# Expert products in a mixture-of-experts block: gate and up laid side by side, 512 columns wide

## The chip, the cores and the metric

One NeuronCore of a Trainium2 chip runs the whole program. Its engines work side by side and wait for each other by semaphores: TensorE (PE) multiplies matrices and writes into PSUM banks of 512 columns, VectorE (DVE) and ScalarE (ACT) work elementwise, GpSimd (POOL) does the rest and issues the gathers from DRAM, SyncE (SP) issues the loads. The metric is the device time of one execution in microseconds (us).

## The reference, cut to what matters

The reference is a stack of four attention layers and then a block with a mixture of experts over 256 tokens of 1024 features. Each token goes to 8 of 64 experts. The change touches only the experts' part:

```
hg = jnp.einsum('cd,edf->cef', xc, w_eg)      # gate, D=1024 -> F=256
hu = jnp.einsum('cd,edf->cef', xc, w_eu)      # up,   D=1024 -> F=256
a = jax.nn.silu(hg) * hu * gch[..., None]
return jnp.einsum('cef,efd->cd', a, w_ed)     # down, F=256 -> D=1024
```

## The kernel before, in words

Everything up to the experts (some 888 us) is left as it is by the change. In the experts' part the tokens are sorted into units. Each expert's three matrices lie in DRAM as one row of 3 x 2048 columns per partition: piece 0 is gate, piece 1 is up, piece 2 is down, 1 MB each. There are two kinds of unit, and the routing of this input makes 16 of the first and 22 of the second.

**Big units** (`unit`, up to 128 places of one expert, 16 run, one after the other, each behind a branch in `chain`). A weight piece is loaded in two halves into `eraw`, split by ACT (`hi`, L1847) and DVE (`lo`, L1850) into two parts, and multiplied three times (hi x hi, hi x lo, lo x hi). `wide(u, a, c)` (L1898) makes gate for c = 0 and up for c = 1 from piece c, over all eight row blocks k of 128 features; each matmul has 256 columns. Around the two wide products TensorE turns the former unit's result (`turn`, L1904), adds the unit before that one into the output (`combine`, L1923), multiplies the former unit by its down matrix (`down`, L1917), and turns the next unit's rows (`cols`, L1889). Those rows come by a gather that GpSimd issues (`fetch`, L1882, into `xr`) at the start of the unit ahead of the one that uses them. Order on TensorE: wide 0, turn, combine 0, wide 1, cols 0, combine 1, down 0, cols 1, places, down 1.

**Pairs** (`pair`, two units of at most 64 places side by side in the two column halves of the array, 11 pairs here). The weights are used unsplit. A ring of 11 buffers of 1 MB holds pieces; `load_p(p, j)` loads piece j // 2 of expert j % 2. `wide_p` (L2058) makes gate and then up, 16 matmuls of 256 columns per call, each of which the profile shows as two instructions. `gather_p` (L2049) makes two of the eight row blocks of a later group's input per call, by a product with a one-hot matrix into a PSUM bank, which `copy` moves to `xs` (L273 on ACT, L275 on DVE). `turn_p` (L2064) turns the activation, ACT copies it to `ats` (L2065); `places_p` (L2034, L2036) turns the one-hots, and `down_p` (L2073) multiplies by down. `gather_p`, `turn_p` and `places_p` each take a bank from `tbank`, which hands out two PSUM banks in turn. The experts' part runs under a manual schedule: instructions stand on each engine as they are written, and the framework adds the semaphores that reads and writes of a tile need. In `pair` the gate's `silu` (L2090, ACT) is written behind the gate's product, so that it runs beside the up product, and `av` (L2095, DVE) behind the up product.

Of the kernel before, what the change touches and what calls it, by code (L numbers as in the profile page):

```python
# [13 lines left out]
AF = mybir.ActivationFunctionType  # L14
# [4 lines left out]
P = 128  # L19
S = 256  # L20
D = 1024
KT = D // P
# [3 lines left out]
E = 64  # L26
# [5 lines left out]
def cols_chunk(w, cols, k0=0, nk=8):  # L32

    c = w[k0 * P:(k0 + nk) * P][:, cols]
    return c.reshape(nk, P, c.shape[1]).transpose(1, 0, 2).reshape(P, -1)


def rng(a, n):
    return np.arange(a, a + n)
# [95 lines left out]
def wkey(key, inputs):  # L135
    a = inputs[key]
    return a.reshape(a.shape[-2], a.shape[-1])


def lay_out(inputs):  # L140

    x = {}
    g = {k: np.asarray(v) for k, v in inputs.items()}
    x["w_all"] = np.concatenate(
        [cols_chunk(wkey(key, g), cols, k0, nk).ravel() for _, key, cols, k0, nk in CHUNKS])
    eg = g["w_exp_gate_2"][0].reshape(E, 8, P, 256).transpose(0, 2, 1, 3)
    eu = g["w_exp_up_2"][0].reshape(E, 8, P, 256).transpose(0, 2, 1, 3)
    ed = g["w_exp_down_2"][0].reshape(E, 2, P, D).transpose(0, 2, 1, 3)
    x["w_exp"] = np.concatenate([eg.reshape(E, P, 2048), eu.reshape(E, P, 2048), ed.reshape(E, P, 2048)], axis=2)
    x["x"] = g["x"].reshape(2, P, D)  # L150
    x["pos"] = np.ascontiguousarray(g["positions_2"].reshape(2, P).T)

    def col(a):
        return a.reshape(-1, P).T

    x["cols"] = np.concatenate([
        col(g["c_2"].reshape(-1)),
        col(g["b_ada_2"].reshape(-1)),
        col(g["g_norm1_2"].reshape(-1)),
        col(g["g_norm2_2"].reshape(-1)),  # L160
        g["a_cmp_pos_k"][0].reshape(16, 2, 64).transpose(1, 2, 0).reshape(P, 16),
        g["a_cmp_pos_v"][0].reshape(16, 2, 64).transpose(1, 2, 0).reshape(P, 16),
        np.tile(g["g_na_q_2"].reshape(64, 1), (2, 1)),
        np.tile(g["g_na_k_2"].reshape(64, 1), (2, 1)),
        col(g["g_q_lat_2"].reshape(-1)),
        col(g["g_kv_lat_2"].reshape(-1)),
        np.tile(g["g_mla_q_2"].reshape(-1), 2)[:P].reshape(P, 1),
        np.tile(g["g_mla_k_2"].reshape(-1), 2)[:P].reshape(P, 1),
    ], axis=1)
    x["rows"] = np.concatenate([  # L170
        g["norm_pre"], g["norm_post"], g["g_norm2_2"],
    ], axis=0)
    x["small"] = np.concatenate([g["b_lambda"].reshape(-1), g["b_sub_gain"].reshape(-1), g["e_bias_2"].reshape(-1)])
    x["w2k"] = cols_chunk(wkey("a_cmp_w2_k", g), rng(0, 64), 0, 2)
    x["w2v"] = cols_chunk(wkey("a_cmp_w2_v", g), rng(0, 64), 0, 2)

    rq, cq = np.divmod(np.arange(P), 64)
    j = np.arange(-2, 4)
    ck = np.arange(64)
    dr = j[None, :] - rq[:, None] + 7  # L180
    dc = np.clip(ck[None, :] - cq[:, None], -15, 15) + 15
    rpb = g["na_rpb_2"][0]
    x["na_bias"] = rpb[:, dr[:, :, None], dc[:, None, :]].transpose(1, 0, 2, 3).reshape(P, -1)
    x.update(constants())
    return {k: np.ascontiguousarray(v) for k, v in x.items()}


def constants():
    c = {}
    p = np.arange(P)[:, None]  # L190
    k = np.arange(S)[None, :]
    dist = P + p - k
    big = np.float32(BIG)
    n = np.arange(16)[None, :]
    q = np.arange(P)
    cs = np.clip(q % 64 - 8, 0, 48)[:, None]
    ck = np.arange(64)[None, :]
    inv = (np.float32(10000.0) ** (-np.arange(16, dtype=np.float32) / np.float32(16))).astype(np.float32)
    cmp = [i * P + p - (16 * n + 31) for i in range(2)]

    def put(name, *t):
        c[name] = np.concatenate([np.broadcast_to(a, (P, np.shape(a)[-1])) for a in t], axis=1).astype(np.float32)

    put("consts", np.eye(P), np.where(dist >= 0, dist, big),
        *[np.where((d >= 0) & (n < 15), d, big) for d in cmp],
        np.where(p >= 31, 1.0, 0.0),
        np.where((ck >= cs) & (ck < cs + 16), 0.0, BIG), inv[None])
    put("consts_c", *[np.where((dist >= 0) & (dist % d == 0) & (dist <= w), dist, big) for w, d in ((128, 1), (512, 4), (2048, 16))])
    put("consts_d", np.where(q[:, None] >= q[None, :], -1.0, 0.0), np.full((P, P), -1.0))
    rest = np.where(q >= E, 128.0, 0.0)[None]  # L210
    put("consts_r", np.where(q[:, None] < q[None, :], 1.0, 0.0),
        127.0 - q[None], 127.0 - p, rest, rest.T, rest + 999.0, np.concatenate([np.arange(Kernel.NB), np.arange(Kernel.NS)])[None], p % E)
    put("consts_e", q[None] - 999.0, q[None] % E - 999.0)
    return c
# [18 lines left out]
class Kernel:  # L233
# [1562 lines left out]
    def units(self, num, hn, y):  # L1796
# [3 lines left out]
        nc, tc = self.nc, self.tc  # L1800
# [13 lines left out]
        xs = [mp.tile([P, KT, S], F32, name=f"xs{i}") for i in range(2)]  # L1814
# [6 lines left out]
        sv = mp.tile([P, 256], F32, name="sv")  # L1821
# [30 lines left out]
        def w(j, nk):  # L1852
            return [hl[q][j].rearrange("p (k c) -> p k c", k=nk) for q in range(2)]
# [37 lines left out]
            self.split(x[0], x[1], b.rearrange("p (k n) -> p k n", k=4))  # L1891

        def wide(u, a, c):
            ww = w(c, KT)
            for k in range(KT):
                x = [t[:, k, (u % 2) * P:(u % 2 + 1) * P] for t in self.x]
                for j, (q, p) in enumerate(((0, 0), (0, 1), (1, 0))):
                    nc.tensor.matmul(a[:, c * 256:(c + 1) * 256], x[p], ww[q][:, k, :],  # L1898
                                     start=(k == 0 and j == 0), stop=(k == KT - 1 and j == 2))

        def turn(u):
# [18 lines left out]
        def combine(u, hf, t=None):  # L1920
            for tt in range(2):
                for p in range(2):
                    nc.tensor.matmul(y[tt][hf], (t or pt[u % 5])[:, tt * P:(tt + 1) * P], yo[p][:, 512 * hf:512 * hf + 512],  # L1923
                                     start=False, stop=False, skip_group_check=True)

        def unit(u):
# [8 lines left out]
            if u:  # L1935
                for h in range(2):
                    hi(2, h)
                    lo(2, h)
                    load(u, 2, h)
            a = self.abank()  # L1940
            wide(u, a, 0)
            if u:
                turn(u - 1)
# [4 lines left out]
            for h in range(2):  # L1948
                hi(0, h)
                lo(0, h)  # L1950
                load(u + 2, 0, h)
            wide(u, a, 1)
            if not u:
                places(0)
# [60 lines left out]
        def ring(p, j):  # L2015
            return R[(6 * p + j) % 11]

        def load_p(p, j):
            nc.sync.dma_start(ring(p, j), weights(NB + 2 * p + j % 2, j // 2))
# [31 lines left out]
            self.copy(xs[g % 2][:, k0:k0 + 2, :], b.rearrange("p (k n) -> p k n", k=2), eng)  # L2051

        def wide_p(p, a, c):
            t = [ring(p, 2 * c + e).rearrange("p (k c) -> p k c", k=KT) for e in range(2)]
            for k in range(KT):
                for e in range(2):
                    s = p % 2 * P + 64 * e
                    nc.tensor.matmul(a[64 * e:64 * e + 64, c * 256:(c + 1) * 256], xs[p // 2 % 2][:, k, s:s + 64], t[e][:, k, :],  # L2058
                                     start=(k == 0), stop=(k == KT - 1))

        def turn_p(p):
            b = self.tbank()
            for f in range(2):
                nc.tensor.transpose(b[:, f * P:(f + 1) * P], av[:, f * P:(f + 1) * P], self.ident)  # L2064
            nc.scalar.activation(ats[p % 2], b[:, :S].rearrange("p (f t) -> p f t", f=2), AF.Copy)  # L2065
# [11 lines left out]
        def pair(p, more):  # L2077
            g, i = divmod(p, 2)
            steps = [4 * i, 4 * i + 2] if more and g + 1 < NP // 2 else []
            gath = lambda e: steps and gather_p(g + 1, steps.pop(0), e)  # L2080
            if more:
                for j in range(5):
                    load_p(p + 1, j)
                if i == 0 and g + 2 < NP // 2:
                    onehot_p(g + 2)
            a = self.abank()
            wide_p(p, a, 0)
            if more:
                load_p(p + 1, 5)
            nc.scalar.activation(sv, a[:, 0:256], AF.Silu)  # L2090
            if p:
                combine(p - 1, 0)
            gath("a")
            wide_p(p, a, 1)
            V.tensor_tensor(av, a[:, 256:512], sv, OP.mult)  # L2095
            if p:
                combine(p - 1, 1)
            turn_p(p)
            gath("v")
            places_p(p)  # L2100
            for hf in range(2):
                down_p(p, hf)
            if not more:
                for hf in range(2):
                    combine(p, hf)
# [101 lines left out]
```

## Time and profile before

| | before |
|---|---|
| median of 3 runs (lowest, highest) | 1284.9 us (1281.04, 1289.26) |
| the profiled execution's own time | 1287.51 us |
| its span, first to last instruction | 1285.8 us |
| PE busy | 1214.1 us, 94% |
| PEld (weight load, beside PE) busy | 1040.0 us, 81% |
| DVE busy | 950.7 us, 74% |
| ACT busy | 695.0 us, 54% |
| DMA in the pairs (1120.3 to 1259.6 us) | 395 GB/s, engines busy 0.97 of the time |

The share of busy time is an average over stages with different limits, so each stage is read by itself. The time of a matmul row is that of the whole passage through the array; what a matmul costs in a row of matmuls is the distance from its start to the next one's start.

### The profile page before, as it was taken

What the parts mean: (1) busy time and instruction counts of PE and PEld (TensorE: products, weight loads), DVE (VectorE), ACT (ScalarE), POOL (GpSimd) and SP (SyncE); (2) the same over time, 40 slices, a digit from 0 to 9 for tenths busy, and PEclk for the clock granted to TensorE, in tenths of its full rate; (3) what the DMA queues carried; (4) which work ended last, traced back from release to release, by engine and by line L of the source; (5) the groups of instructions that cost most, each with busy time, mean ns of one, the idle gap of its engine ahead of it and who ended that gap; (6) DMA issues with size and microseconds to landing.
All of it is one profiled execution on the core that took longest, in us unless ns stands there. A gap on an engine that the chain in (4) does not pass through costs nothing. (4 is left out here: it accounts for less than half of the span.)

```text
span 1285.8 us, 23661 instructions
## 1 busy us (share of the span) xinstructions
PE 1214.1 (94%) x8366; PEld 1040.0 (81%) x8366; DVE 950.7 (74%) x2363; ACT 695.0 (54%) x1509; POOL 223.2 (17%) x295
## 2 busy tenths in 40 slices
PE   5899998999989999999989999989899998999996
PEld 5888876998879987999878898878889887666663
DVE  6977889879997788888689689878889887211123
ACT  5667785456645554468665555543767766211111
POOL 2034411001100110002100000023335344011100
PEclk9988998999989999999999999999999999899998
DMA  8461205664357644866444235335888887999991
GB/s 298 165 235 34 99 34 166 252 238 158 109 188 283 226 139 144 320 249 250 148 170 169 85 115 174 131 145 195 324 310 286 296 306 271 381 418 403 414 403 48
DMA packets 54802, 282.19 MB, mean 219 GB/s; under 512 B 5920, under 2 KB 6720, under 8 KB 29952
## 3 DMA queue, kind: packets, MB, share of 16 engines
q1 hardware_dynamic: 48784, 261.98, 55.1%
q0 software_dynamic: 4000, 15.44, 3.4%
q10 hardware_dynamic: 1872, 2.99, 0.7%
q8 instruction: 72, 1.18, 0.4%
q14 instruction: 74, 0.61, 0.1%
HBM read 278.27 MB, written 2.11 MB: 218 GB/s over the span
## 5 line engine op out<-in xcount | busy, mean ns | idle before, releaser
L351 ACT ACTIVATE hi<-raw 128x512 fp32r<-128x512 f32 (+4 forms) x452 | 247.1, 604 | 126.7 <-PE acc L415 58.6
L358 DVE TENSOR_TENSOR lo<-raw,hi 128x512 fp32r<-128x512 f32 (+5 forms) x446 | 286.5, 670 | 28.0 <-ACT hi L351 26.9
L415 PE MATMUL acc<-x,hi 128*128 128x256 f32 x1440 | 276.8, 291 | 0.0
L415 PEld LDWEIGHTS acc<-x,hi 128*128 128x128 f32 x1440 | 227.7, 194 | 9.7 <-issue 7.9
L415 PE MATMUL acc<-x,lo 128*128 128x256 f32 x720 | 206.3, 287 | 3.5 <-DVE lo L358 3.5
L415 PEld LDWEIGHTS acc<-x,lo 128*128 128x128 f32 x720 | 139.3, 194 | 5.0 <-DVE lo L358 4.3
L1850 DVE TENSOR_TENSOR elo<-eraw,ehi 128x1024 fp32r<-128x1024 f32 x99 | 118.0, 1228 | 8.8 <-ACT ehi L1847 8.7
L453 PE MATMUL acc<-hi,x 128*128 128x256 f32 x544 | 109.0, 296 | 6.6 <-DVE x L279 2.4
L1847 ACT ACTIVATE ehi<-eraw 128x1024 fp32r<-128x1024 f32 x100 | 102.2, 1054 | 15.9 <-DMA eraw<-in_w_exp_dram 9.7
L453 PEld LDWEIGHTS acc<-hi,x 128*128 128x128 f32 x544 | 90.1, 200 | 9.6 <-DVE x L279 3.5
L1898 PE MATMUL acc<-ehi,x 128*128 128x256 f32 x512 | 95.0, 286 | 2.4 <-ACT ehi L1847 2.4
L1898 PEld LDWEIGHTS acc<-ehi,x 128*128 128x128 f32 x512 | 82.7, 194 | 5.1 <-ACT ehi L1847 2.7
L453 PE MATMUL acc<-lo,x 128*128 128x256 f32 x272 | 79.2, 292 | 0.3 <-DVE lo L358 0.3
L642 ACT ACTIVATE p<-sb,m 128x256 f32<-128x256 f32 (+1 forms) x136 | 61.2, 452 | 29.9 <-DVE m L641 25.1
L1909 DVE SCALAR_TENSOR_TENSOR yo<-acc,gc,yo 128x512 fp32r<-128x512 f32 x52 | 38.9, 748 | 49.9 <-ACT yo L1908 49.9
L1898 PE MATMUL acc<-elo,x 128*128 128x256 f32 x256 | 73.1, 286 | 0.8 <-DVE elo L1850 0.8
L2095 DVE TENSOR_TENSOR av<-acc,sv 128x256 f32<-128x256 f32 x11 | 4.7, 425 | 87.1 <-PE acc L2058 87.1
L387 DVE SCALAR_TENSOR_TENSOR macc<-raw,sc,macc 128x512 f32<-128x512 f32 x84 | 63.5, 756 | 6.4 <-DMA raw<-in_w_all_dram 4.9
L1908 ACT ACTIVATE yo<-acc,gc 128x512 fp32r<-128x512 f32 x52 | 35.8, 688 | 51.3 <-PE acc L2073 42.1
L583 PE MATMUL acc<-hi,g 128*128 128x512 f32 x192 | 63.1, 400 | 0.0
L453 PEld LDWEIGHTS acc<-lo,x 128*128 128x128 f32 x272 | 54.4, 200 | 0.5 <-DVE lo L358 0.5
L278 ACT ACTIVATE x<-t 128x512 fp32r<-128x512 f32 x50 | 29.6, 596 | 45.8 <-PE t L1889 34.3
(597 smaller groups left out, 2800.6 us busy)
## 6 DMA issues: line engine op xcount, KB each, us to landing
raw<-in_w_all_dram SPq DMA_DIRECT2D x128, 1024.0 KB, 4.9
eraw<-in_w_exp_dram SPq DMA_DIRECT2D x102, 512.0 KB, 5.9
ring<-in_w_exp_dram SPq DMA_DIRECT2D x36, 1024.0 KB, 8.6
eraw<-in_w_exp_dram SPq DMA_DIRECT2D x16, 1024.0 KB, 8.8
first<-in_w_exp_dram SPq DMA_DIRECT2D x12, 1024.0 KB, 8.7
gain<-in_rows_dram POOLq DMA_DIRECT2D x8, 512.0 KB, 4.0
raw<-in_w_all_dram SPq DMA_DIRECT2D x2, 832.0 KB, 4.5
nab<-in_na_bias_dram POOLq DMA_DIRECT2D x1, 1536.0 KB, 6.7
```

What stands on the lines that cost most here:

```text
L351: self.nc.scalar.activation(hi[:, c], raw[:, c], AF.Copy)
L358: eng.tensor_tensor(lo[:, c], raw[:, c], hi[:, c].bitcast(F32), OP.subtract)
L387: nc.vector.scalar_tensor_tensor(self.macc, w[:, k, :], sc, self.macc, op0=OP.mult, op1=OP.add)
L415: self.nc.tensor.matmul(av[:, i, :], w[:, k, c], x[u][:, k, :], start=(k == 0 and j == 0), stop=(k == nk - 1 and j == 2))
L453: self.nc.tensor.matmul(a[:, :n], self.x[u][:, k, tt * P:(tt + 1) * P], ww[:, k, :], start=(k == 0 and j == 0), stop=(k == KT - 1 and j == 2))
L583: self.nc.tensor.matmul(a, gt[u][:, 4 * i + k, tt * P:(tt + 1) * P], ww[:, k, :], start=(i == 0 and k == 0 and j == 0), stop=(i == 1 and k ...
L642: nc.scalar.activation(out, sb[:, :n], AF.Exp, bias=m, scale=-1.0, accum_out=ssum)
L1847: nc.scalar.activation(half(hl[0][j], j, h), half(raw[j], j, h), AF.Copy)
L1850: V.tensor_tensor(half(hl[1][j], j, h), half(raw[j], j, h), half(hl[0][j], j, h).bitcast(F32), OP.subtract)
L1898: nc.tensor.matmul(a[:, c * 256:(c + 1) * 256], x[p], ww[q][:, k, :], start=(k == 0 and j == 0), stop=(k == KT - 1 and j == 2))
L1908: nc.scalar.activation(yo[0][:, c], a, AF.Copy, scale=g)
L1909: V.scalar_tensor_tensor(yo[1][:, c], a, g, yo[0][:, c].bitcast(F32), op0=OP.mult, op1=OP.subtract)
```

## The change: what it does

In DRAM, gate and up of an expert stand side by side: row block k is one run of 512 columns (256 of gate, 256 of up). Piece 0 is now the row blocks 0 to 3 of both, piece 1 the row blocks 4 to 7 of both; piece 2 (down) and all sizes and loads stay. `wide` and `wide_p` with c = 0 add up the row blocks 0 to 3 and with c = 1 the blocks 4 to 7, in matmuls of 512 columns, half as many. Gate is finished only when c = 1 is. In `pair` the `silu` moves behind the second wide product, and the second gather (`gath("v")`) moves ahead of `turn_p`.

```
-    eg = g["w_exp_gate_2"][0].reshape(E, 8, P, 256).transpose(0, 2, 1, 3)
-    eu = g["w_exp_up_2"][0].reshape(E, 8, P, 256).transpose(0, 2, 1, 3)
+    gu = np.concatenate([g["w_exp_gate_2"][0], g["w_exp_up_2"][0]], axis=2).reshape(E, 8, P, 512).transpose(0, 2, 1, 3)
...
         def wide(u, a, c):
-            ww = w(c, KT)
-            for k in range(KT):
+            ww = w(c, 4)
+            for k in range(4 * c, 4 * c + 4):
...
-                    nc.tensor.matmul(a[:, c * 256:(c + 1) * 256], x[p], ww[q][:, k, :],
+                    nc.tensor.matmul(a, x[p], ww[q][:, k % 4, :],
...
         def wide_p(p, a, c):
-            t = [ring(p, 2 * c + e).rearrange("p (k c) -> p k c", k=KT) for e in range(2)]
-            for k in range(KT):
+            t = [ring(p, 2 * c + e).rearrange("p (k c) -> p k c", k=4) for e in range(2)]
+            for k in range(4 * c, 4 * c + 4):
...
-                    nc.tensor.matmul(a[64 * e:64 * e + 64, c * 256:(c + 1) * 256], xs[p // 2 % 2][:, k, s:s + 64], t[e][:, k, :],
+                    nc.tensor.matmul(a[64 * e:64 * e + 64, :], xs[p // 2 % 2][:, k, s:s + 64], t[e][:, k % 4, :],
...
             wide_p(p, a, 0)
             if more:
                 load_p(p + 1, 5)
-            nc.scalar.activation(sv, a[:, 0:256], AF.Silu)
             if p:
                 combine(p - 1, 0)
             gath("a")
             wide_p(p, a, 1)
+            nc.scalar.activation(sv, a[:, 0:256], AF.Silu)
             V.tensor_tensor(av, a[:, 256:512], sv, OP.mult)
             if p:
                 combine(p - 1, 1)
+            gath("v")
             turn_p(p)
-            gath("v")
             places_p(p)
```

The order of the built programs shows the second place on TensorE. The names with numbers are tiles: `t_10639` and `t_10640` are the two PSUM banks of `tbank`, and in brackets stands the engine that the instruction waits for. In a pair of the kernel before, from the end of the second combine to the first down product (the six other gather rows are left out at "..."):

```order
L1923 MATMUL o_10300<-yo1_10694,pt0_10668 128x512
L2064 MATMUL t_10640<-consts_75,av_10682 128x128 [waits DVE_49]
L2064 MATMUL t_10640<-consts_75,av_10682 128x128
L2049 MATMUL t_10639<-ps1_10302,hn0_10283 128x256 [waits Activation_49]
L2049 MATMUL t_10639<-ps1_10302,hn1_10284 128x256
...
L2034 MATMUL t_10640<-consts_75,ps0_10301 128x128 [waits Activation_49]
L2034 MATMUL t_10640<-consts_75,ps0_10301 128x128
L2036 MATMUL t_10640<-gsp_10437,ps0_10301 128x8 x2
L2073 MATMUL acc_10642<-eraw2_10652,ats1_10692 64x512 [waits DMAHW2_49]
```

The same place of the changed kernel (its lines are one lower):

```order
L1922 MATMUL o_10300<-yo1_10694,pt0_10668 128x512
L2048 MATMUL t_10640<-ps1_10302,hn0_10283 128x256
L2048 MATMUL t_10640<-ps1_10302,hn1_10284 128x256
...
L2063 MATMUL t_10639<-consts_75,av_10682 128x128 [waits DVE_49]
L2063 MATMUL t_10639<-consts_75,av_10682 128x128
L2033 MATMUL t_10640<-consts_75,ps0_10301 128x128 [waits DVE_49]
L2033 MATMUL t_10640<-consts_75,ps0_10301 128x128
L2035 MATMUL t_10640<-gsp_10437,ps0_10301 128x8 x2
L2072 MATMUL acc_10642<-eraw2_10652,ats1_10692 64x512 [waits DMAHW2_49,Activation_49]
```

The gather now fills bank `t_10640` ahead of the turn, and `places_p` (L2033) takes the same bank next: it waits for DVE, which copies the gather out of that bank; before, it waited for ACT, which copied the turned activation out of it. On ACT, in a pair of the kernel before:

```order
L2090 ACTIVATE sv<-acc 128x256 [waits DVE_49,PE_49,Activation_49]
L273 ACTIVATE xs_10667<-t 128x512 [waits PE_49]
L2065 ACTIVATE ats_10692<-t 128x256 [waits PE_49]
L1908 ACTIVATE yo_10693<-acc,gc_10674 128x512 [waits DVE_49,PE_49,Activation_49]
L1908 ACTIVATE yo_10693<-acc,gc_10674 128x512 [waits PE_49,Activation_49]
```

And of the changed kernel:

```order
L272 ACTIVATE xs_10667<-t 128x512 [waits PE_49]
L2093 ACTIVATE sv<-acc 128x256 [waits DVE_49,PE_49,Activation_49]
L2064 ACTIVATE ats_10692<-t 128x256 [waits PE_49]
L1907 ACTIVATE yo_10693<-acc,gc_10674 128x512 [waits DVE_49,PE_49,Activation_49]
L1907 ACTIVATE yo_10693<-acc,gc_10674 128x512 [waits PE_49,Activation_49]
```

The copy of the first gather now stands ahead of the `silu`. DVE, POOL and SP hold the same instructions in the same order in both kernels; TensorE's differ in the wide products and in the place shown.

## Rows read from the trace of the kernel before

**Rows 1.** Stretches: bounds, length, busy us of PE, PEld, DVE, ACT, POOL, clock, DMA.

```profile
917.00:1085.30 168.30, 164.94 (x1118) 149.84 (x1117) 146.18 (x203) 118.96 (x163) 71.33 (x43) 1.00 0.85 299
1120.30:1259.60 139.30, 139.30 (x990) 86.57 (x990) 28.63 (x63) 24.69 (x45) 12.59 (x30) 1.00 0.97 395
```

**Rows 2.** The chain that ended last, one pair: start us, us, what.

```profile
1120.27 3.58 PE acc L2058 x32
...
1125.93 3.60 PE acc L2058 x32
...
1130.67 0.22 PE t L2064 x2
...
1132.18 3.58 PE acc L2073 x16
1135.76 3.58 PE acc L2058 x32
```

**Rows 3.** All waits of PE from 1105.5 to 1259.6: total us, times, longest.

```profile
PE t L2064 <- DVE av L2095: 0.6, 1, 0.6
```

**Rows 4.** Timeline of a pair, from the turn on: start us, us, engine, line.

```profile
1161.48 0.38 PE L2064 MATMUL t<-consts,av 128*128 128x128 f32 x2
1161.61 1.20 PE L2049 MATMUL t<-ps,hn 128*128 128x256 f32 x8
...
1161.89 0.39 ACT L2065 ACTIVATE ats<-t 128x256 f32<-128x256 f32 x1 [4.35 <-PE t L2064]
1162.65 0.38 PE L2034 MATMUL t<-consts,ps 128*128 128x128 f32 x2
...
1162.92 0.69 DVE L275 COPY xs<-t 128x512 f32<-128x512 f32 x1 [1.84 <-PE t L2049]
```

**Rows 5.** Timeline of the next pair: silu, and the end of the up product.

```profile
1170.43 0.39 ACT L2090 ACTIVATE sv<-acc 128x256 f32<-128x256 f32 x1 [2.88 <-PE acc L2058]
...
1175.93 0.73 PE L1923 MATMUL s<-yo,pt 128*128 128x512 f32 x2
...
1176.15 0.42 DVE L2095 TENSOR_TENSOR av<-acc,sv 128x256 f32<-128x256 f32 x1 [7.81 <-PE acc L2058]
```

**Rows 6.** Timeline of PE in a big unit: wide 0, turn, cols 0, down 0, cols 1.

```profile
988.64 0.40 PE L1898 MATMUL acc<-ehi,x 128*128 128x256 f32 x2
...
991.51 0.38 PE L1904 MATMUL t<-consts,av 128*128 128x128 f32 x2
...
995.57 0.66 PE L1889 MATMUL t<-consts,xr 128*128 128x128 f32 x4
...
997.00 0.62 PE L1917 MATMUL acc<-ehi,at 128*128 128x512 f32 x2
...
998.37 0.60 PE L1889 MATMUL t<-consts,xr 128*128 128x128 f32 x4
```

**Rows 7.** Timeline of POOL in that unit: the gather, and what ended the idle time.

```profile
989.50 1.67 POOL L1882 DMA_INDIRECT xr<-hrow,ix  x1 [7.01 <-PE acc L1917]
```

**Rows 8.** All gathers (L1882): count, who waited (us, times), landing.

```profile
L1882 POOL DMA_INDIRECT xr<-hrow,ix x15: 1019/1672/1675, 900.9 to 1075.9; - x15
...
  PEld t L1889: 5.8, 12
...
DMA to landing us min/median/max: 5.9/6.3/7.2
```

**Rows 9.** Timeline of PE: two waits in big units.

```profile
904.72 0.50 PE L1898 MATMUL acc<-ehi,x 128*128 128x256 f32 x2 [2.45 <-ACT ehi L1847]
...
1020.74 0.66 PE L1889 MATMUL t<-consts,xr 128*128 128x128 f32 x4 [0.87 <-DMA xr<-hrow,ix]
```

**Rows 10.** Stretches behind these two waits, columns as in rows 1.

```profile
904.70:909.80 5.10, 4.32 (x21) 4.12 (x22) 5.07 (x6) 4.94 (x6) 0.00 (x0) 0.67 0.85 302
1019.80:1024.00 4.20, 3.33 (x20) 2.77 (x20) 2.45 (x4) 2.01 (x4) 0.00 (x0) 1.00 0.95 342
```

More of the change, by code (lines that the diff above doesn't have):

```diff
@@ L145, in lay_out @@
         [cols_chunk(wkey(key, g), cols, k0, nk).ravel() for _, key, cols, k0, nk in CHUNKS])
-    eg = g["w_exp_gate_2"][0].reshape(E, 8, P, 256).transpose(0, 2, 1, 3)
-    eu = g["w_exp_up_2"][0].reshape(E, 8, P, 256).transpose(0, 2, 1, 3)
+    gu = np.concatenate([g["w_exp_gate_2"][0], g["w_exp_up_2"][0]], axis=2).reshape(E, 8, P, 512).transpose(0, 2, 1, 3)
     ed = g["w_exp_down_2"][0].reshape(E, 2, P, D).transpose(0, 2, 1, 3)
-    x["w_exp"] = np.concatenate([eg.reshape(E, P, 2048), eu.reshape(E, P, 2048), ed.reshape(E, P, 2048)], axis=2)
+    x["w_exp"] = np.concatenate([gu.reshape(E, P, 4096), ed.reshape(E, P, 2048)], axis=2)
     x["x"] = g["x"].reshape(2, P, D)
```

## The prediction

> **What bounds the kernel now.** I read the stretches first: they show two stages of different make. In the big units PE is busy 164.9 of 168.3 us, in the pairs 139.3 of 139.3 us [rows 1]. TensorE's share alone doesn't say what sets the time, so I read in each stage which wait ends last.
>
> In the pairs, the chain that ended last runs on PE alone, with a period of 1135.76 - 1120.27 = 15.49 us: two wide products of 3.58 and 3.60, a down product of 3.58, and small work between [rows 2]. In the whole stage PE waited once, 0.6 us, in the first pair, and never for a weight piece [rows 3]. So the pairs are bound by TensorE, and every wait that is put into PE's order there lengthens the run by its full size. The loads keep pace closely (395 GB/s, DMA share 0.97 [rows 1]), but PE doesn't wait for them.
>
> In the big units the reader should look at the gather, not at PE's busy time. GpSimd issues it at 989.50, released by the last down product of the unit before, 0.86 us after PE started the unit at 988.64; PE wants its rows at 995.57, 6.07 us after the issue [rows 6, 7]. A gather takes 5.9 to 7.2 us, in the median 6.3, and PE's weight load waited for 12 of the 15 [rows 8]. So the round is: end of a unit, gather, landing, `cols`, down, end of the unit. The wide products lie beside the gather's flight, not in that round.
>
> **The change part by part.** *Big units, wider matmuls.* Eight triples of 256 columns take 991.51 - 988.64 = 2.87 us, 0.359 each; two triples of 512 columns (down) take 998.37 - 997.00 = 1.37, 0.685 each [rows 6]. So two narrow triples (0.718) become one wide one (0.685): 0.033 us less, and with eight wide triples per unit 0.26 us, which would be 4.2 us over 16 units. But both wide products stand between the unit's start and `cols`. PE would be there 6.93 - 0.26 = 6.67 us after its start, 5.81 us after the issue of the gather, earlier than the fastest landing of 5.9 [rows 6 to 8]. Where PE waits already, the gain goes into a longer wait. Only the three units whose gather was not waited for can gain, 0.8 us at most, and one of the early units stands 2.45 us for `hi`, which takes up what is gained ahead of it [rows 9]. I take -0.5 us; the bounds are 0 and -4.2.
>
> *Pairs, wider matmuls.* Here the trace has both shapes with the same 64-column weights: 32 instructions of 256 columns take 3.58 to 3.60 us and 16 of 512 columns 3.58 [rows 2]. The columns decide, not their number per instruction. I take 0. As the other bound I use the saving of the big units, 0.033 of 0.718 or 4.6%, of 11 x 7.18 us: -3.6 us.
>
> *Pairs, the gather ahead of the turn.* This costs. Before, PE made the turn at 1161.48, the gather at 1161.61 and `places_p` at 1162.65; DVE copied the gather out of its bank from 1162.92 for 0.69, until 1163.61, that is 2.00 us after the gather's start [rows 4]. Nobody waited for that copy, since `places_p` used the other bank. Now `places_p` follows the gather in the same bank, as the order shows, and must wait for the copy. The gather now starts where the turn did, so `places_p` can start 2.00 us after that point; before it started 1162.65 - 1161.48 = 1.17 us after it. PE loses 0.83 us, and the step from DVE's end to PE's start on top, a few hundredths that I leave out. The turn, now between gather and `places_p`, takes 0.13 us and is inside the 2.00. Down and the next pair's products stand behind `places_p` on PE and move by as much. Ten pairs have a second gather (the last has none). Nine of them give 7.5 us. In the first, PE already stood 0.6 us waiting for `av` [rows 3]; the gather now fills that time, which leaves 0.2 us. The bounds of this term are 0 (if another wait covers it) and 10 x 0.83 = 8.3 and the steps.
>
> The Trainium skill speaks for this wait ("PSUM — Partial Sum Buffer", Terms): TensorE writing and VectorE reading one bank at once is an error, so the copy has to end first. Without an overlap the term is 7.7 us; if `places_p` could write beside the copy, it would be 0. No row shows such an overlap.
>
> *Pairs, silu behind the second product.* After the end of the up product (1175.93) DVE started `av` at 1176.15, 0.22 later [rows 5]. Now ACT's `silu` (0.39) comes between: 0.22 + 0.39 + 0.42 = 1.03 us and two steps between engines until the turn may start. In the nine middle pairs the combine (from 1129.53 to 1130.67, 1.14 us [rows 2]) and the gather behind it cover that. In the last pair the combine alone does, to within 0.1 us. `ats` is ready 1161.89 + 0.39 - 1161.48 = 0.80 us after the turn's start [rows 4]; the gather holds PE for 1162.65 - 1161.61 = 1.04 us ahead of the turn, so `ats` comes 1.84 us after the gather's start, ahead of the 2.00 at which `places_p` is released, and costs nothing beside it. If the copy were out of the way, `ats` would be late next.
>
> *Loads.* Sizes, count and order are as before, and buffers come free in the same order. A pair of 15.49 + 0.83 = 16.32 us needs less bandwidth than one of 15.49 us.
>
> Sum: 7.5 + 0.2 - 0.5 = +7.2 us. On the profiled execution's own time that is 1287.5 + 7.2 = 1294.7. That execution was 2.6 us above the median of the runs (1284.9), so the median I expect is 1292.1 us, 0.6% more than before.
>
> **The rivals.**
> *The wider products pay in full and nothing new is waited for.* Then -4.2 in the big units and -3.6 in the pairs: 1284.9 - 7.8 = 1277.1. For it speaks that there are half as many matmuls; against it the 12 waited gathers and the equal 3.58 us in the pairs. The Trainium skill ("TensorE: Matmul & The Clock Gate", Back-to-back issue gap) goes further: 131 ns per sustained matmul at 512 columns against 81 at 128. This trace does not agree: 512 columns cost 0.685 / 3 = 0.228 us here [rows 6].
>
> *The new wait is hidden.* If the loads were the true pace of the pairs (share 0.97), a wait of PE would only let the pieces land earlier: -0.5 us, 1284.4. Against it: PE waited for no piece in the whole stage [rows 3]. It would need a wait for pieces of 0.83 us per pair, and there is none.
>
> *Much slower: the clock.* A wait of 2.45 us in an early unit was followed by a stretch at clock 0.67, partly at the lower of the two levels, 1.2 GHz [rows 9, 10]. Such a stretch costs 5.1 x 0.33 = 1.7 us. If each of ten new waits brought one, the time would be 1292.1 + 17 = 1309. Against it: after a wait of 0.87 us, the size of the new one, the clock stayed at 1.00 [rows 9, 10]. [...]
>
> **How the numbers follow.** The forecast (0.5 to 1% slower, mostly by the copy) 0.74; the hidden wait 0.12; full pay 0.06; the clock 0.08. The predicted time is that of the forecast, 1292.1. Its own range is from 1288 (with the 3.6 of the pairs gained) to 1298 (all ten waits in full, no gain in the units, and the 4 us by which runs of before lie above their median). For 8 in 10 I go down to 1286, toward the hidden wait, and up to 1299. What differs by less than about 1% (12.8 us) a measurement of this kernel can't tell from no change. Faster than that: 0.03, half of full pay. Slower: 0.08 from the clock and 0.05 from the forecast's upper end, 0.13. Within: 0.84.
>
> **What would show it.** Right: among PE's waits in the pairs a row of `places_p` (L2033) for DVE's `xs` copy, some 0.8 us, ten times; a period of 16.3 us; wide products of 3.58 us in 16 instructions; in the big units a longer wait of `cols` for the gather with an unchanged round of 12.5 us, (1075.9 - 900.9) / 14 [rows 8]. Wrong: a pair of 15.5 us or less (the wait hidden, or the products faster); big units shorter by 0.2 us each (the gather follows PE and was no bound); a clock under 0.95 in the pairs.

## The result, and the profile after

The changed kernel took 1292.3 us in the median (1289.8 to 1297.2), the kernel before 1286.5 in the same rounds: a ratio of 1.0056 with a 95% interval of 1.0031 to 1.0080. It is slower by a little more than half a percent: the interval leaves out 1, and the difference lies below the 1% that the prediction took as the least that can be told from no change. The profiled execution has a span of 1290.0 us against 1285.8.

The page of the changed kernel, its head, shows that TensorE has 736 matmuls fewer and is as busy as before, 1212.1 us against 1214.1:

```profile
span 1290.0 us, 22159 instructions
## 1 busy us (share of the span) xinstructions
PE 1212.1 (94%) x7630; PEld 992.2 (77%) x7630; DVE 951.1 (74%) x2363; ACT 694.9 (54%) x1509; POOL 224.8 (17%) x295
```

Where the time went shows only by stages. The stretches of the changed kernel, cut at the start of the first and of the last wide matmul of the big units and of the first wide and the last down matmul of the pairs (columns as in [rows 1]):

```profile
0.00:894.20 894.20, 845.04 (x5861) 757.11 (x5862) 738.43 (x2035) 523.17 (x1264) 128.71 (x206) 0.98 0.48 173
894.20:1082.20 188.00, 180.47 (x871) 145.52 (x870) 161.56 (x229) 132.48 (x179) 76.89 (x47) 0.98 0.87 309
1082.20:1103.40 21.20, 15.42 (x60) 10.60 (x58) 11.48 (x19) 9.67 (x13) 3.32 (x8) 0.84 0.70 258
1103.40:1277.70 174.30, 168.22 (x833) 77.65 (x834) 33.96 (x75) 28.87 (x53) 13.37 (x32) 1.00 0.88 359
1277.70:1290.00 12.30, 2.98 (x12) 1.35 (x8) 5.63 (x8) 0.69 (x1) 2.49 (x2) 0.80 0.25 90
```

Cut in the same way, all profiles of this study read as follows (us). The first stretch holds the same instructions in every one of them.

| profile | before the units | big units | between | pairs | tail | span |
|---|---|---|---|---|---|---|
| before | 892.0 | 189.8 | 24.1 | 167.4 | 12.5 | 1285.8 |
| before, second profile | 889.3 | 189.6 | 20.7 | 167.5 | 12.5 | 1279.6 |
| changed | 894.2 | 188.0 | 21.2 | 174.3 | 12.3 | 1290.0 |
| changed, second profile | 896.0 | 188.1 | 20.8 | 174.0 | 12.4 | 1291.4 |
| turn first | 897.0 | 187.3 | 21.0 | 168.3 | 12.7 | 1286.4 |
| before, gather first | 897.5 | 190.1 | 22.9 | 174.5 | 12.5 | 1297.4 |
| places first | 895.7 | 189.0 | 21.0 | 173.1 | 12.3 | 1291.2 |
| copy in halves | 888.9 | 189.2 | 21.4 | 175.9 | 12.5 | 1287.9 |
| turn first, 256 columns | 893.3 | 189.7 | 23.3 | 169.5 | 12.3 | 1288.1 |
| turn first, early gather | 895.8 | 184.7 | 23.0 | 168.5 | 12.6 | 1284.7 |
| before, early gather | 893.0 | 186.1 | 20.7 | 167.2 | 12.0 | 1279.1 |

The pairs are 6.9 us longer, the big units 1.8 us shorter. The other stretches vary between executions of the same kernel by as much as the two kernels differ there: 889.3 to 892.0 and 20.7 to 24.1 us for the kernel before. A difference of two spans would have mixed all that into the change.

The chain of the changed kernel, one pair, answers to [rows 2]; a pair now takes 1150.30 - 1134.08 = 16.22 us instead of 15.49:

```profile
1134.08 3.56 PE acc L2057 x16
...
1139.71 3.58 PE acc L2057 x16
1143.29 0.66 PE s L1922 x2
1143.95 0.47 PE o L1922 x2
1144.42 0.97 PE t L2048 x8
...
1145.42 0.70 DVE xs L274
...
1146.16 0.44 PE t L2033 x2
1146.60 0.12 PE t L2035 x2
1146.72 3.58 PE acc L2072 x16
1150.30 1.84 PE acc L2057 x7
```

DVE stands in a chain that was TensorE's alone: behind the second gather (L2048) comes DVE's copy of it (L274), and only then `places_p` (L2033). The wide products take 3.56 and 3.58 us in 16 instructions, where 32 took 3.58 and 3.60. The timeline of that place answers to [rows 4]:

```profile
1144.26 1.12 PE L2048 MATMUL t<-ps,hn 128*128 128x256 f32 x8
...
1145.22 0.38 PE L2063 MATMUL t<-consts,av 128*128 128x128 f32 x2
1145.42 0.69 DVE L274 COPY xs<-t 128x512 f32<-128x512 f32 x1 [1.16 <-PE t L2048]
1145.63 0.38 ACT L2064 ACTIVATE ats<-t 128x256 f32<-128x256 f32 x1 [1.84 <-PE t L2063]
1146.16 0.44 PE L2033 MATMUL t<-consts,ps 128*128 128x128 f32 x2 [0.56 <-DVE xs L274]
```

All waits of PE in the pairs, which answer to [rows 3], are now ten times this one (a matmul's row runs on to its modelled end, so the idle time is shorter than the shift of the starts):

```profile
PE t L2033 <- DVE xs L274: 5.6, 10, 0.6
PE acc L2057 <- issue: 0.3, 1, 0.3
```

In the big units the gathers answer to [rows 8]: one more was waited for, and the waits of the weight load grew from 5.8 to 10.6 us.

```profile
  PEld t L1888: 10.6, 13
...
DMA to landing us min/median/max: 4.6/6.2/7.3
```

### The profile page after: what moved, and what is told of

The parts are those of the page before. It is cut to its first block, busy times and chain, and to the rows that moved or that the text cites. A ratio compares the mean times of both kernels' runs of the same rounds, so it can differ in the third digit from the quotient of the medians.

```text
span 1290.0 us, 22159 instructions
## 1 busy us (share of the span) xinstructions
PE 1212.1 (94%) x7630; PEld 992.2 (77%) x7630; DVE 951.1 (74%) x2363; ACT 694.9 (54%) x1509; POOL 224.8 (17%) x295
## 5 line engine op out<-in xcount | busy, mean ns | idle before, releaser
L1897 PE MATMUL acc<-ehi,x 128*128 128x512 f32 x256 | 81.4, 399 | 2.8 <-ACT ehi L1846 2.8
L1897 PEld LDWEIGHTS acc<-ehi,x 128*128 128x128 f32 x256 | 48.8, 192 | 13.8 <-ACT ehi L1846 3.1
L1856 POOL TENSOR_SCALAR pm<-consts_e,place 128x128 fp32r<-128x128 f32 x32 | 53.1, 1666 | 7.5 <-PE t L1865 7.1
```

What stands on the lines that cost most here:

```text
L1856: eng.tensor_scalar(pm[u // 2 % 2][:, tt, u % 2], self.iota, self.place[:, tt, u:u + 1], None, op0=OP.is_equal)
L1897: nc.tensor.matmul(a, x[p], ww[q][:, k % 4, :], start=(k == 0 and j == 0), stop=(k == KT - 1 and j == 2))
```

## The experiments

My theory was that the pairs pay because `places_p` now takes the bank out of which DVE still copies the second gather, and that the big units gain next to nothing because the gather sets their round. The rivals: the late `silu` or the new pieces cost the time in the pairs; the width alone explains the big units.

**The turn ahead of the second gather again.** One edit on the changed kernel:

```
-            gath("v")
             turn_p(p)
+            gath("v")
             places_p(p)
```

> The changed kernel with the turn ahead of the second gather again, as in the kernel before; the new layout, the 512-column products and the silu behind the second product stay. Theory (places_p waits for DVE's copy because the gather has taken the place of the turn): that wait goes, a pair takes 15.5 us instead of 16.2, the turn waits for av by no more than 0.1 us, and the time falls by some 7 us to between 1284 and 1287, a ratio of about 0.999 to the kernel before. Rival (the silu behind the second product, or the half-row pieces, make the pairs longer): a pair stays at 16.0 us or more and the time at about 1292, ratio 1.005.

Measured: 1285.7 us, ratio 0.9987 (0.9967 to 1.0007). The pairs' stretch is 168.3 us. The chain of a pair of this kernel:

```profile
1151.16 3.56 PE acc L2057 x16
...
1161.51 0.33 PE t L2063 x2
1161.84 0.96 PE t L2048 x8
1162.80 0.22 PE t L2033 x2
1163.02 0.12 PE t L2035 x2
1163.14 3.58 PE acc L2072 x16
1166.72 3.56 PE acc L2057 x15
```

DVE's copy is gone from the chain, and a pair takes 15.56 us (first wide products start at 1151.16 and 1166.72). It stays 0.07 us above the kernel before, because the turn takes 0.33 us in the chain instead of 0.22: `av` comes about 0.1 us late behind the `silu`, as expected. In the first pair PE's wait for `av` grew from the 0.6 us of [rows 3]:

```profile
PE t L2063 <- DVE av L2094: 1.0, 1, 1.0
```

Of the 6.9 us of the pairs' stretch 0.9 remain, which come with the late `silu`; the rest was the place of the gather.

**The same move alone, on the kernel before.** Old layout, 256 columns, early `silu`:

```
+            gath("v")
             turn_p(p)
-            gath("v")
             places_p(p)
```

> The kernel before with one edit: the second gather ahead of the turn. Layout, 256-column products and the early silu are those of before. Theory: DVE's copy of the gather ends last ahead of places_p in nine pairs of eleven and more, a pair takes 16.2 to 16.3 us, the first pair about 0.1 us more than before, and the time rises by some 7 us to 1293 or 1294, ratio 1.0055. Rival (the late silu is what costs in the changed kernel): a pair stays at 15.5 us, ratio 1.000.

Measured: 1294.0 us, ratio 1.0049 (1.0024 to 1.0074); pairs of 16.27 us, a stretch of 174.5. Its chain shows the same link:

```profile
1151.60 0.98 PE t L2049 x8
...
1152.60 0.70 DVE xs L275
...
1153.35 0.44 PE t L2034 x2
1153.79 0.12 PE t L2036 x2
1153.91 3.58 PE acc L2073 x16
```

So this one edit, without layout, width or `silu`, costs what the whole change costs in the pairs.

**`places_p` ahead of the second gather.** The bank is then no longer shared with a gather that is being copied:

```
-            gath("v")
-            turn_p(p)
             places_p(p)
+            gath("v")
+            turn_p(p)
```

> The changed kernel with places_p ahead of the second gather, so that places_p does not share the bank with a gather whose copy is under way. Theory: the copy no longer holds anything, but the turn stands last and down has to wait for ats, which is ready 0.80 us after the turn's start; from the end of the combine to down it is then 0.35 + 1.04 + 0.85 = 2.2 us against 2.3 in the changed kernel and 1.5 in the kernel before, so a pair takes 16.1 to 16.2 us and the time stays at about 1292, ratio 1.005. Rival (ats would not be late next): a pair of 15.5 us, ratio 0.999.

Measured: 1292.7 us, ratio 1.0052 (1.0026 to 1.0079); pairs of 16.11 us. The wait went to where the prediction had put it next, to `ats`:

```profile
1148.16 0.23 PE t L2063 x2
...
1148.41 0.39 ACT ats L2064
...
1148.85 3.65 PE acc L2072 x16
```

**The copy in halves.** In `gather_p` the copy of the second gather was cut in two, 256 columns on ACT and 256 on DVE:

```
+            v = b.rearrange("p (k n) -> p k n", k=2)
...
+                for i, e in enumerate("av"):
+                    self.copy(xs[g % 2][:, k0 + i:k0 + i + 1, :], v[:, i:i + 1, :], e)
```

> The changed kernel, with the copy of the second gather cut in two halves, one on DVE and one on ACT at the same time (256 columns each, about 0.4 us instead of 0.7). Theory (the end of that copy releases places_p): PE's wait of places_p falls from 0.56 to about 0.25 us; ACT makes its half ahead of ats, so ats ends last next and gives part of it back; a pair takes 15.9 to 16.1 us instead of 16.23 and the time falls by 1.5 to 3 us below that of the changed kernel, ratio 1.003 to 1.004 to the kernel before. Rival (the wait has nothing to do with how long the copy takes): the pair stays at 16.2 us.

Measured: 1296.5 us, ratio 1.0082 (1.0051 to 1.0114); pairs of 16.39 us. The expectation was wrong: the two halves didn't run at the same time.

```profile
1157.26 0.97 PE t L2050 x8
...
1158.26 0.39 ACT xs L272
1158.65 0.02 issue
1158.68 0.44 DVE xs L274
...
1159.16 0.44 PE t L2033 x2
```

In the built program DVE's half waits for ACT alone:

```
L2101 TENSOR_TENSOR av<-acc,sv 128x256 [waits Activation_49]
L274 COPY xs_10667<-t 128x256 [waits Activation_49]
```

The framework lets one engine after the other read the bank. The Trainium skill ("PSUM — Partial Sum Buffer", Terms) counts two engines that read one bank at once among the errors; the program keeps apart what the page forbids, so no run here shows what would happen otherwise. The run still tells the theories apart, in the other direction than meant: the copy grew from 0.70 to 0.39 + 0.02 + 0.44 = 0.85 us, and the pair by 16.39 - 16.23 = 0.16. The pair follows the copy's length almost one for one. The pairs explain only 1.6 us (175.9 against 174.3) of the 4 us by which the median lies above that of the changed kernel; the rest is within what the two intervals, which overlap, leave open.

**The gather issued early, 512 and 256 columns.** In both kernels the `fetch` moves from the start of the next unit to right behind the places that it needs:

```
-            if 2 <= u + 1 < n:
-                fetch(u + 1)
...
             if u + 2 < n:
                 places(u + 2 if u else 1)
+                fetch(u + 2)
```

First on the changed kernel with the turn first, then on the kernel before:

> The changed kernel with the turn first again (as e1) and each big unit's gather issued at the end of the unit two ahead, right behind the places it needs, instead of at the start of the next unit: some 2.5 us earlier. Theory (the gather, not TensorE, sets the round of the big units, so that the 512-column products gain nothing there): PE no longer waits for the rows, the round falls from 12.4 to about 11.8 us, that is by the wait of 0.4 to 0.7 us, and the time to about 1277, ratio 0.992. Rival (TensorE or DVE sets the round): it stays at 12.4 and the time at that of e1, ratio 0.999.

> The kernel before (old layout, 256-column products, old pair) with the gather issued early, as in e4. Theory: the round falls by PE's wait alone, from 12.5 to about 12.05 us, and stays 0.26 us longer than in e4, which is what 24 matmuls of 512 columns save against 48 of 256 once nothing hides it; time about 1281, ratio 0.995. Rival (512 columns save nothing even there): the rounds of e4 and e5 are equal. Second rival (the gather sets no round): 12.5 us and ratio 1.000.

Measured: 1281.9 us, ratio 0.9965 (0.9943 to 0.9988), with 512 columns; 1281.6 us, ratio 0.9977 (0.9957 to 0.9997), with 256. The starts of the gathers of three units, first with 512 columns, then with 256:

```profile
966.87 1.01 POOL L1881 DMA_INDIRECT xr<-hrow,ix  x1 [9.34 <-DVE ix L1867]
...
978.53 1.00 POOL L1881 DMA_INDIRECT xr<-hrow,ix  x1 [9.32 <-DVE ix L1867]
...
990.18 1.02 POOL L1881 DMA_INDIRECT xr<-hrow,ix  x1 [9.32 <-DVE ix L1867]
```

```profile
965.72 1.02 POOL L1882 DMA_INDIRECT xr<-hrow,ix  x1 [9.58 <-DVE ix L1868]
...
977.61 1.00 POOL L1882 DMA_INDIRECT xr<-hrow,ix  x1 [9.57 <-DVE ix L1868]
...
989.51 1.02 POOL L1882 DMA_INDIRECT xr<-hrow,ix  x1 [9.57 <-DVE ix L1868]
```

In the units that wait for no gather the round is 11.65 us with 512 columns and 11.90 with 256, within 0.02 us from unit to unit. With the gather out of the way TensorE sets the round, and the wider products save 0.25 us per unit, where the prediction had 0.26. The rivals of both expectations fall.

The move in time was smaller than expected. The gather starts not 2.5 but 0.47 us earlier, 0.39 us after the first wide product of its unit instead of 0.86, released now by DVE's `ix`; the larger part came from its landing, 5.1 us after the issue in the median instead of 6.2. The unit that starts near 990, in the changed kernel, and the same unit's first wide product with the early gather, whose issue at 990.18 stands above:

```profile
989.81 0.62 PE L1897 MATMUL acc<-ehi,x 128*128 128x512 f32 x2
...
990.67 1.67 POOL L1881 DMA_INDIRECT xr<-hrow,ix  x1 [6.70 <-PE acc L1916]
```

```profile
989.79 0.62 PE L1897 MATMUL acc<-ehi,x 128*128 128x512 f32 x2
```

With 256 columns the time is as expected (1281); with 512 the gain is less than expected (1277). There two gathers still landed late, and those two units took 12.93 and 13.11 us; the second unit stood 4.30 us for `hi`, against 2.83 in the changed kernel; and the profiled execution, at 1286.4 us, was the slowest of the twelve, so what it shows need not hold for the median. All waits of PE for the gather in that kernel:

```profile
PE t L1888 <- DMA xr<-hrow,ix: 2.3, 2, 1.2
```

The version with 512 columns, the turn first and the early gather is the fastest that I ran by its ratio, below both kernels. By the median the 256-column one with the early gather is 0.3 us lower, and the two intervals overlap, so which is better stays open: in the profiles the wide one gains 1.4 us in the big units (184.7 against 186.1) and loses 1.3 in the pairs (168.5 against 167.2).

**256 columns in the new layout.** As with the turn first, but each wide product made as two matmuls side by side:

```
-                    nc.tensor.matmul(a, x[p], ww[q][:, k % 4, :],
+                    for h in range(2):
+                        nc.tensor.matmul(a[:, 256 * h:256 * h + 256], x[p], ww[q][:, k % 4, 256 * h:256 * h + 256],
```

> As e1 (new layout, turn first, silu late), but each wide product of 512 columns made as two of 256 columns side by side, 48 instead of 24 per big unit, with one start for the bank. Theory: the pairs take the same 15.5 us and the big units a round of 12.4 to 12.5 us, since the gather sets it, so the time is that of e1 to within 2 us, ratio 0.999 to 1.001. Rival (the width brought the 1.8 us that the big units of the changed kernel are shorter by): the stretch of the big units goes back from 187.3 to 189.7 us and the pairs grow with it by up to 3.6 us, ratio 1.003.

Measured: 1288.7 us, ratio 1.0025 (1.0001 to 1.0049). Against the theory, the big units go back to 189.7 us from 187.3, and the ratio is nearer to the rival's 1.003. The pairs are 169.5 us against 168.3, 0.1 us per pair. But the twelve units from the fourth on, which wait for the gather, don't go back: they take 12.31 us in the mean, against 12.34 with 512 columns. The difference lies in the others: the first unit (6.95 against 6.74), the second, which stands for `hi` (15.56 against 14.38, the shortest of all profiles), the third (12.65 against 11.69) and the last. So this run shows no gain of the width behind the gather. Besides, the five profiles with 512 columns and the late gather spread from 187.3 to 189.2 us, and this kernel was compared with the lowest of them.

**Both kernels once more**, for second profiles.

> The kernel before once more, for a second profile of it: what of the stretch before the big units, of the big units and of the stretch between them and the pairs changes from one execution to the next with nothing changed. Theory: the stretch before the big units varies by some 2 us and the one between units and pairs by up to 3 us (low clock and waits for code), so that of the differences between the first two profiles only the pairs' +6.9 us belongs to the change. Rival: these stretches repeat to within 0.3 us, and the 2.9 us that the changed kernel saved between units and pairs are its own.

> The changed kernel once more, for a second profile. Theory: the pairs repeat to 0.1 us (16.23 each, the stretch 174.3 us), and the stretch before the big units (894.2 in the first profile) and the mean unit of the big units (12.27) differ by up to 4 us and 0.1 us from the first profile, as they did between two profiles of the kernel before (892.0 and 889.3; 12.37 and 12.42). Rival: the mean unit of 12.27 us repeats to 0.02 us and is then a gain of the wide products of its own.

Their stretches stand in the table. The pairs repeat to 0.3 us (167.4 and 167.5; 174.3 and 174.0), the big units to 0.2. From the fourth unit on, the mean time from one first wide product to the next, from the timelines, was 12.27 and 12.30 us in the changed kernel and 12.37 and 12.42 before; four profiles leave open whether the change itself brought that 0.1 us. In the stretch between units and pairs the granted clock was 0.72 and 0.92 before and 0.84 in the changed kernel; no profile shows that code was waited for there, as I had supposed.

## Why the prediction was right, point by point

**The place of the gather.** Predicted: 0.83 us in each of nine pairs, 0.2 in the first, 7.7 in all, by DVE's copy. Measured: 0.73 us (16.22 against 15.49), 0.1 in the first (14.36 against 14.27), 6.9 in all, with ten waits of `places_p` for that copy. The mechanism is shown by the chain, by taking the move back, and by making the move alone. The move alone cost 16.27 - 15.49 = 0.78 us per pair, 7.1 in the stretch, so the term itself was sized 0.05 us too high per pair. The gather became shorter: from its start to the next instruction it took 1145.22 - 1144.26 = 0.96 us, not the 1.04 of [rows 4], so the copy started sooner and `places_p` could start 1146.16 - 1144.26 = 1.90 us after it, not 2.00. Against it, the transposes behind the wait took some 0.05 us more until the down product. The rest of the way to 0.73 is what the wider products save in a pair.

**Wider products in the pairs.** Predicted: nothing. Measured: 3.56 and 3.58 us instead of 3.58 and 3.60, so 0.4 us over 22 products, a ninth of the -3.6 that I had as a bound. In the new layout with 256 columns a pair took 15.66 us against 15.56, 0.1 us more; this is the most that the width can be said to bring there.

**Wider products in the big units.** Predicted: 0.26 us per unit, hidden but for -0.5 us in all. The first number is right where the gather doesn't cover it (0.25). The second was too small: -1.8 us in the first profile. Five profiles with 512 columns and the late gather average 188.3 us and four with 256 columns 189.8, so about -1.5 us. From the fourth unit on, where the gather is waited for, those averages are 12.33 and 12.38 us per unit, which is 0.5 us over 12 units; single profiles spread as far (12.27 to 12.38 and 12.31 to 12.42), so this part isn't shown. The first two units together take 22.4 us in both averages: the first is 0.24 us shorter, and the second, which stands for `hi`, is that much longer, as I had expected, though the second varies by more than 1 us between profiles. The third, whose rows PE mostly doesn't wait for, is 0.5 us shorter in the average and 0.3 in the first profiles (11.62 against 11.93). The remaining 0.4 lies in the last unit and is in part the cut's doing, which falls at a start of a matmul: behind it PE waits 0.52 us for the gather instead of 0.26 in the first profiles.

**silu behind the second product.** Predicted: covered, by at most 0.1 us exposed. Measured with the turn first: 0.1 us in the turn of the middle pairs, and 0.3 in the first pair (14.57 against 14.27), where I hadn't priced it. In the changed kernel the gather covers it in ten pairs and no wait for `av` is left there. In the last pair, which has no gather, the turn started 1.22 us after the combine instead of 1.03, and the pair took 14.08 us instead of 13.88: 0.2 us, where I had 0.1.

**The rivals.** The hidden wait fell: PE waited ten times, though the loads still keep 0.88 of the DMA engines busy. The clock rival fell: the pairs ran at 1.00 with ten new waits in them. Nor does the length of a wait alone decide it: at the place of [rows 9] PE stood 2.70 us for `hi` with the places first and 2.65 in the second profile of the changed kernel, longer than the 2.45 there, and the clock from 905 to 910 us was 1.00 in both.

**The sum.** It came out somewhat too high (+7.2 us predicted, +5.8 in the medians). Both errors point the same way: the pairs cost 6.9 us instead of 7.7, and the big units gained 1.0 us more than predicted. That the predicted time, 1292.1 us, lies 0.2 us from the measured median is luck: it was added to a median before of 1284.9, and in the rounds of the comparison the kernel before took 1286.5, which made up for the error.

## What to carry to other kernels

When a step is moved on an engine whose banks rotate by turns, look at which bank the next step takes: here a swap of two lines gave the waiting step the bank whose evacuation was the longest and the latest, and that cost 7 us, while the products that the change was about gave some 1.5 in the big units and 0.4 in the pairs. A gain beside a transfer is worth little until the transfer comes earlier: the same 0.25 us per unit appeared in full once the gather landed in time. Read spans by stages, since untouched stretches vary by more than such an edit.

## What the runs showed that I had not expected

Written at the end of the unit instead of the start of the next, the gather instruction itself takes GpSimd 1.0 us instead of 1.67 ([rows 7] and the rows above), and it lands after 5.1 us in the median instead of 6.2 (with 256 columns 4.9 instead of 6.3); the two one-hots behind it take 1.3 us instead of 3.7. In the late form the one-hots run beside DVE's `lo` splits, in the early form for 0.7 of the 1.3 us beside its scaling of the down product; the timeline of GpSimd, first in the changed kernel, then with the early gather:

```profile
992.36 3.72 POOL L1856 TENSOR_SCALAR pm<-consts_e,place 128x128 fp32r<-128x128 f32 x2
```

```profile
991.22 1.29 POOL L1856 TENSOR_SCALAR pm<-consts_e,place 128x128 fp32r<-128x128 f32 x2
```

The Trainium skill ("GPSIMD Engine Reference", Specifications) says that GpSimd shares its SBUF interface with VectorE and contends with instructions that have two inputs in SBUF, as `lo` has. The durations of the one-hots agree with it, but no run here changed that alone. That of the gather instruction doesn't follow from it: the short one (990.18 to 991.20) ran beside a `lo` split from 990.22 on.

A copy that is cut over two engines became longer than the whole one, 0.85 against 0.70 us, since the halves read one bank in turn.
